# The order of three closing stores in an average pool, and a wait that one of them gets

## Chip, cores, metric

One core of a Trainium2 chip. The metric is the device time of one execution in microseconds (us).

## The reference

```python
# x: float32 (8, 32, 32, 32, 32); result: float32 (8, 32, 16, 16, 16)
window = x[:, :, 2*i:2*i+2, 2*j:2*j+2, 2*k:2*k+2]
result[:, :, i, j, k] = np.mean(window, axis=(-3, -2, -1))
```

It reads 33.55 MB, writes 4.19 MB, and adds eight numbers for each result. The kernel is a stream of DMA (copies between HBM, the chip's large memory, and the on-chip memory) with additions beside it.

## The kernel before

Ten units of rows are loaded one after the other on one DMA queue, reduced on VectorE in three steps (depth, width, height), and collected in two output buffers. Three stores on the same queue end the program.

```python
    def pool_unit(buf, t, k0, kb):
        od = kb // 8
        a = buf.rearrange("p (o dd e) -> p o dd e", o=od, dd=2)
        b = buf[:, :od * 1024]
        nc.vector.tensor_add(                                  # depth sum (line 65)
            out=b.rearrange("p (o e) -> p o e", o=od), in0=a[:, :, 0], in1=a[:, :, 1])
        # ... width sum (line 69), height sum and scale into obuf[t] (line 72)

    for t, k, kb in plan:                                      # units 0 to 9
        # ...
        nc.sync.dma_start(out=buf, in_=src)                    # loads 0 to 9
        pool_unit(buf, t, k, kb)

    nc.sync.dma_start(out=ov, in_=obuf[0])                     # store A: 2 MB, units 0 to 3

    for queue, k, n, kb in [
        (nc.sync, 0, 4, 3),                                    # store B: 1.5 MB, units 4 to 7
        (nc.sync, 12, 2, 2),                                   # store C: 0.5 MB, units 8 and 9
    ]:
        queue.dma_start(out=of[...], in_=obuf[1][...])         # cut
```

Load n is called Ln below; L8 and L9 have 2 MB each. B has 12 KB in each of the 128 partitions. After the program is compiled, the kernel also rewrites the access patterns of some DMAs and the closing of the program; the argument doesn't rest on that.

## Time and profile before

| | before |
|---|---|
| time, median of 3 runs | 91.96 us (91.9 to 92.06) |
| DMA queue | 99.2% of sixteen engines' span, 36.44 MB in the span |
| VectorE busy | 64.3 us of 86.5 (74%) |
| A issued / landed | 55.80 / 85.51 us |
| B issued / landed | 76.57 / 89.22 us |
| C issued / landed | 84.96 / 90.46 us |
| landing of L8, L9 | 75.26, 80.59 us |

Each of the sixteen DMA engines works through its own part of every transfer, in the order in which the transfers were issued. The packet records fit this: L9 is 64 packets of 32 KB, in four rounds of sixteen, one per engine, and the first packet of A starts at 79.72, when the last one of L9 has long started (78.47). A transfer has landed when its semaphore, the counter that others wait for, says so. The span of the profile ends with the last instruction; the stores land after it. Times in the text are counted from the start of the span.

### The profile page before, as it was taken

The page shows a single profiled execution, that of the slowest core. Times are in us where ns is not written, and L with a number is a line of the kernel's source. Part 1 is how long each engine was busy: PE and PEld are TensorE (multiplying, and loading weights), DVE is VectorE, ACT ScalarE, POOL GpSimd, SP SyncE. Part 2 cuts the span into 40 slices and gives each one's busy share as a digit, 9 for nine tenths or more (in the row PEclk, how much of TensorE's full clock was granted, in tenths as well). Part 3 has the DMA queues.
Part 4 walks back from the last instruction along what each step waited for, and adds up shares of the span by engine and source line. Part 5 has one row for each costly group of instructions (what it writes and reads, how often), then busy time and mean ns, then how long its engine had stood idle before and what let it go on. Part 6 is the DMA issues. An engine that isn't in the chain of part 4 may idle for free.

```text
span 86.5 us, 90 instructions
## 1 busy us (share of the span) xinstructions
DVE 64.3 (74%) x40; POOL 0.2 (0%) x4
## 2 busy tenths in 40 slices
DVE  0000049992999749992999999799689949999992
POOL 0000000000000000000000000000000000000000
DMA  8979998899979999899889998889988899899999
GB/s 242 424 333 455 485 485 379 379 455 485 485 318 424 470 485 424 364 424 606 364 364 409 591 455 364 364 364 523 568 364 364 364 485 424 349 439 303 432 439 402
DMA packets 1264, 36.44 MB, mean 421 GB/s; under 512 B 176, under 2 KB 176, under 8 KB 176
## 3 DMA queue, kind: packets, MB, share of 16 engines
q1 hardware_dynamic: 1264, 36.44, 99.2%
HBM read 33.55 MB, written 4.19 MB: 436 GB/s over the span
## 4 chain that ended last, share of the span: by engine, by line
DMA 71%; DVE 26%; issue 0%; SPq 0%; DVEq 0%
DMA tin<-in_x_dram 71%; DVE tin L65 14%; DVE tin L69 8%; DVE obuf L72 4%; SPq L85 0%; DVE dummy L72 0%; DVEq L106 0%
## 5 line engine op out<-in xcount | busy, mean ns | idle before, releaser
L65 DVE TENSOR_TENSOR tin<-tin 128x4096 f32<-128x4096 f32 (+2 forms) x10 | 35.7, 3570 | 19.9 <-DMA tin<-in_x_dram 19.9
L69 DVE TENSOR_TENSOR tin<-tin 128x2048 f32<-128x2048 f32 (+2 forms) x10 | 18.6, 1865 | 0.3
L72 DVE CUSTOM_DVE_ANT_1 obuf<-tin 128x1024 f32<-128x1024 f32 (+2 forms) x10 | 10.1, 1011 | 0.3
L72 DVE DVE_READ_ACCUMULATOR2_ANT dummy<- 128x1 f32 x10 | 0.8, 82 | 0.0
L200 POOL MEMSET const-bfloat16-1.0<- 128x1 bf16 x1 | 0.1, 101 | 0.0
L200 POOL MEMSET const-uint8-127<- 128x1 uint8 x1 | 0.1, 101 | 0.0
L200 POOL MEMSET const-float32-0.0<- 128x1 f32 x1 | 0.1, 99 | 0.2 <-issue 0.2
L200 POOL MEMSET const-float32-1.0<- 128x1 f32 x1 | 0.1, 99 | 0.0
## 6 DMA issues: line engine op xcount, KB each, us to landing
tin<-in_x_dram SPq DMA_DIRECT2D x4, 4096.0 KB, 25.6
tin<-in_x_dram SPq DMA_DIRECT2D x4, 3072.0 KB, 34.5
tin<-in_x_dram SPq DMA_DIRECT2D x2, 2048.0 KB, 25.7
out_dram<-obuf SPq DMA_DIRECT2D x1, 2048.0 KB, 29.7
out_dram<-obuf SPq DMA_DIRECT2D x1, 1536.0 KB, 12.6
out_dram<-obuf SPq DMA_DIRECT2D x1, 512.0 KB, 5.5
```

The lines of the kernel that those rows point to most:

```text
L65: nc.vector.tensor_add(out=b.rearrange("p (o e) -> p o e", o=od), in0=a[:, :, 0], in1=a[:, :, 1])
L69: nc.vector.tensor_add(out=c, in0=bv[:, :, 0], in1=bv[:, :, 1])
L72: nc.vector.tensor_tensor_reduce(out=obuf[t][:, o0:o0 + od * 256].rearrange("p (j k) -> p j k", k=16), in0=cv[:, :, 0], in1=cv[:, :, 1], s ...
L200: nc = _bacc.Bacc("TRN2", target_bir_lowering=False, num_devices=1)
```

## The change

The intent as I read it: A has been ready since unit 3 and lies in the queue behind the last loads. The change lets the stores come only when the loads are nearly through. B goes first, since it depends on unit 7, and its wait is raised by one VectorE count (one step of the semaphore that VectorE raises). For that count to exist in the right place, the depth sum of unit 8 is cut into two instructions. A stands behind B and so gets into the queue late as well.

```diff
-        nc.vector.tensor_add(
-            out=b.rearrange("p (o e) -> p o e", o=od), in0=a[:, :, 0], in1=a[:, :, 1])
+        bv = b.rearrange("p (o e) -> p o e", o=od)
+        cuts = (0, 1, od) if split else (0, od)
+        for o0, o1 in zip(cuts, cuts[1:]):
+            nc.vector.tensor_add(out=bv[:, o0:o1], in0=a[:, o0:o1, 0], in1=a[:, o0:o1, 1])
...
-        pool_unit(buf, t, k, kb)
-    nc.sync.dma_start(out=ov, in_=obuf[0])
-    for queue, k, n, kb in [(nc.sync, 0, 4, 3), (nc.sync, 12, 2, 2)]:
-        queue.dma_start(out=of[...], in_=obuf[1][...])
+        pool_unit(buf, t, k, kb, split=k == 96 and t == 1)
+    for k, n, kb in [(0, 4, 3), (12, 2, 2)]:
+        nc.sync.dma_start(out=of[...], in_=obuf[1][...])
+        if k == 0:
+            nc.sync.dma_start(out=ov, in_=obuf[0])
...
+    n, store = next(... first store of the program ...)
+    waits = [
+        copy.replace(w, wait_value=w.wait_value + 1) if w.ant_name.startswith("DVE") else w
+        for w in store.sync_info.on_wait]
+    program[n] = copy.replace(store, sync_info=mybir.SyncInfo(
+        on_wait=waits, on_update=store.sync_info.on_update))
```

## The prediction

> **What bounds the kernel now.** I read the page first, its DMA share and its chain, then the order of instructions, then stretches of the DMA stream cut at the borders between transfers, and last the single packet records.
>
> The page says that the sixteen DMA engines are full from end to end:
>
> ```profile
> DMA  8979998899979999899889998889988899899999
> ...
> q1 hardware_dynamic: 1264, 36.44, 99.2%
> HBM read 33.55 MB, written 4.19 MB: 436 GB/s over the span
> DMA 71%; DVE 26%; issue 0%; SPq 0%; DVEq 0%
> ```
>
> One queue moves everything and takes 99.2% of sixteen engines' span; the chain lies to 71% on loads. VectorE is busy 74%, so its waits are waits for loads. The 26% of DVE in the chain is an artefact of where the span stops: it ends with the last instructions at 86.5 us, while the records of the stores go on (last landing 90.46 us in the trace). What ends the run is the last packet of the DMA stream.
>
> The tail on the instruction side, from the order of instructions in time:
>
> ```profile
> 55.80 0.58 SPq L89 DMA_DIRECT2D out_dram<-obuf  x1
> ...
> 76.46 2.29 DVE L65 TENSOR_TENSOR tin<-tin 128x2048 f32<-128x2048 f32 x1
> 76.57 8.96 SPq L96 DMA_DIRECT2D out_dram<-obuf  x2
> ```
>
> Call the last two loads L8 and L9 (2 MB each), the 2 MB store A, the 1.5 MB store of 12 KB a partition B, the 0.5 MB store C. A is issued at 55.80, straight behind L9 (55.28); B at 76.57, when unit 7 is reduced; C at 84.96. The page gives issue to landing: 29.7 for A, 12.6 for B, 5.5 for C, so they land near 85.5, 89.2 and 90.5. The trace's landings are L8 75.26, L9 80.59, A 85.51, B 89.22, C 90.46. The steps are 5.33, 4.92, 3.71 and 1.24 us. A, B and C run at 426, 424 and 423 GB/s with no gap. L9 is the odd one: the same 2 MB as A, but 0.4 us more. Stretches of the stream show it (columns: stretch, its length, VectorE and GpSimd busy, clock, DMA share, GB/s of the packets that start in it):
>
> ```profile
> 62.00:69.30 7.30, 6.08 (x4) 0.00 (x0) 1.00 1.00 431
> 69.30:74.20 4.90, 3.78 (x2) 0.00 (x0) 1.00 1.00 428
> 74.20:79.70 5.50, 5.43 (x5) 0.00 (x0) 1.00 0.99 381
> 79.70:84.55 4.85, 4.75 (x6) 0.00 (x0) 1.00 1.01 432
> ```
>
> The rows are load 7, L8, L9 and A. Only L9 falls, to 381 GB/s, with the engines counted as busy throughout. The packet records say where: of 640 packets of 32 KB, 605 take 1.21 to 1.24 us; the sixteen first of the run take 1.31 to 2.00, and the only other slow ones are three started at 76.7 to 76.9 (1.31 to 1.53) and the sixteen last of L9, one per engine (1.43 to 1.95, mean 1.71). Store packets that follow are all of one length (0.611, 0.460, 0.159 us). So 1.71 - 1.23 = 0.48 us, plus (0.30 + 0.08 + 0.15)/16 = 0.03 for the three, about 0.5 in all, is lost per engine where the stream turns from reading HBM to writing it. It is the only loss in the stream after its opening, hence all that this change can win.
>
> **What the Trainium skill says.** "DMA: Bandwidth & Descriptors", section "Two DMAs through the same engine are not ordered": descriptors of one queue start in order but are pipelined, and an engine's read and write sides are separate queues. The trace agrees that order is kept (no store packet precedes its engine's last load packet). That a store waiting in the queue may already be reading while the last load is being written is the reading I take from it; the 0.5 us fits, but is no proof. Same page, "Latency and other measured facts": first byte some 0.6 us after a hardware-generated issue. Here the first load, issued at 0.00, has its first packets at 1.02 to 1.26 on fourteen engines and 1.65 and 1.89 on two; the measurement decides. "Perfetto Trace Analysis", section "DMA Instruction — HWDGE (DVE, Sync)": the issue seen in the profile starts once its semaphores are satisfied, and data movement is not in it. It agrees: B's 0.62 us issue starts 0.02 after the reduction's semaphore, its data moves eight us later. "VectorE: DVE Perf Modes", section "The TRN2 errata — SBUF-src ops pay a fixed extra latency per instruction": an fp32 add of N columns takes (N+151)/0.96 ns. Here 2048 columns take 2284 ns (formula 2291) and 1024 take 1225 ns (1224), so it agrees.
>
> **The change, part by part.**
>
> *Order.* The stores go B, A, C instead of A, B, C. Bytes and descriptors are the same. At the steady packet lengths above, eight packets an engine each, A takes 4.89, B 3.68, C 1.27, whichever is first. By itself: 0.
>
> *Time of issue.* This is the real part. A is no longer put in the queue at 55.80, because it now stands behind B. B waits for one VectorE count more, the first half of unit 8's depth sum. Unit 7's count comes at 76.55, and half the sum, 1024 columns, is about 1.21 us (line 65 takes 4426, 3358 and 2284 ns for 4096, 3072 and 2048 columns, so about 1071 ns a thousand, and 1213 for 1024). B is issued at 76.55 + 1.21 = 77.76, give or take 0.07. A follows 0.62 later, at 78.4.
>
> *Does the queue run dry?* With the opening's 1.02 to 1.26 us (two engines 1.65, 1.89) from issue to first packet, B's packets could begin at 78.78 to 79.02, on two engines at 79.4 and 79.65. L9's last packets start at 78.07 to 78.47; at 1.23 us they would end at 79.30 to 79.70. B then comes 0.05 to 0.6 us before the engine is free: just in time on most, with nothing to spare on the two slow ones. A has B's 3.68 us in front of it. C is needed when B and A are through, after 79.5 + 3.68 + 4.89 = 88.1.
>
> *VectorE.* The split makes 2284 into 2 x 1213 = 2426 ns, so 0.14 more, and a semaphore step of 0.02 to 0.03. C goes out at 84.96 + 0.17 = 85.13 with its engines taken until 88: 3 us of slack, hidden.
>
> *Sum.* If nothing of the store is in the queue while L9's last packets are filled, up to 0.50 comes back. B still comes somewhat before the end of L9 and some loss will stay, and its own first packet may have to fill an empty pipe. I count about two thirds: 0.50 x 0.65 = 0.33, with the split hidden. 91.96 - 0.33 = 91.63.
>
> **The rivals.**
>
> 1. *The turn costs what it costs.* The 0.5 us comes from changing direction (reads of HBM drained, writes begun), not from an early store. Then it is paid at any issue time: 91.9 to 92.0. For it: the opening packets too take 0.1 to 0.8 us too long, so filling the pipe costs such an amount when nothing is ahead. Against it: the late part is the last load packet, whose landing is really late, not the first store packet.
> 2. *The queue runs dry.* If B needs over 1.6 us to its first packet (its 3 KB rows make four times the write descriptors), all engines stand idle for the difference. At 2 us that is some 0.3 us idle on top of a cleared turn, a time of 91.8 to 92.0; if the turn is paid as well, 92.3. For it: the two slow engines of the opening. Against it: the delay is chosen at half of a sum and not a whole one, which suggests that somebody sought this edge.
> 3. *The issue of B disturbs the loads.* B's descriptors are made at 76.57 to 77.19, just before the three slow packets end. If that slows the loads, a later issue only shifts it: no change, 91.96. Against it: the issues at 20.1, 29.8, 39.5, 49.2, 55.3 and 55.8 have no slow packet after them.
> 4. *All of it comes back:* 91.96 - 0.51 = 91.45. There is nothing else to win: 37.75 MB at the steady 430 GB/s are 87.8 us, and the rest lies in the opening and the closing, which are untouched.
>
> **Range and chances.** The four ways span 91.4 to 92.3; the three runs of before spread by 0.16. I put 0.55 on a gain of 0.2 to 0.5, 0.3 on no change and 0.15 on a loss: 91.63, eight times in ten 91.3 to 92.05. Two per cent is 1.84 us, over three times what the stream loses at all, so faster by that is out; a dry queue of 1.84 us would take 3.5 us from issue to first packet. 0.01, 0.98, 0.01.
>
> **What would show it.** In the changed profile B's issue should stand near 77.8 and A's near 78.4; the two half sums at 1.2 us each; C's issue near 85.1 with a shorter issue to landing, near 5.0. The stretch of L9 should go back from 381 to over 410 GB/s and its landing from 80.59 to about 80.2, and the last landing from 90.46 to about 90.1. It is wrong if L9's last packets are again 1.7 us long with B issued at 77.8 (rival 1 or 3), or if they are short but a gap, or long first packets of B, stand behind them (rival 2). The idle time of VectorE should not move before 76 us.

## More of the kernel before

All runs told here were at a granted clock of 1.00. Every kernel was timed on the same chip and in the same rounds as the kernel before; the groups of runs were on different chips, on which the kernel before took 91.91 to 91.97 us.

One way of cutting the trace has to be known for what follows. The view of stretches adds up the packets that start in a stretch, so its GB/s depend on where the stretch is cut. The fair cut for a transfer is from its own first packet to the first packet of the next one. For L9 in the kernel before this is 74.28 to 79.72 (columns: stretch, length, VectorE, GpSimd, clock, DMA share, GB/s):

```profile
74.27:79.71 5.44, 5.37 (x5) 0.00 (x0) 1.00 1.00 386
```

## The result

| | before | after |
|---|---|---|
| time, median of 6 runs | 91.93 us (91.74 to 92.09) | 91.29 us (91.27 to 91.31) |
| ratio of the fast runs | | 0.993 (95%: 0.9917 to 0.9943) |
| landing of L8, L9 | 75.26, 80.59 | 75.22, 80.11 |
| last landing | 90.46 | 89.90 |

A ratio here is the mean time of one kernel's fast runs over that of the other's in the same rounds, so not quite the ratio of the medians. The change is worth 0.64 us, 0.7%, clear of the noise and inside the 2%. The predicted 91.63 is 0.34 too high, and the measured time lies 0.01 under the range.

The instructions of the changed kernel from unit 8 on, in order of time (start, length, engine, line, operation):

```profile
76.41 2.48 DVE L68 TENSOR_TENSOR tin<-tin 128x1024 f32<-128x1024 f32 x2
77.66 0.62 SPq L93 DMA_DIRECT2D out_dram<-obuf  x1
78.33 0.58 SPq L98 DMA_DIRECT2D out_dram<-obuf  x1
...
85.11 0.57 SPq L93 DMA_DIRECT2D out_dram<-obuf  x1
```

B is issued at 77.66 (predicted 77.76), A at 78.33 (78.4), C at 85.11 (85.13). The page gives their ways from issue to landing:

```profile
out_dram<-obuf SPq DMA_DIRECT2D x1, 2048.0 KB, 10.3
out_dram<-obuf SPq DMA_DIRECT2D x1, 1536.0 KB, 6.2
out_dram<-obuf SPq DMA_DIRECT2D x1, 512.0 KB, 4.8
```

A was 29.7 us under way and is now 10.3; all but some five of these are waiting in the queue. The stream itself, cut at the first packets of L8, L9, B, A and C:

```profile
69.50:74.40 4.90, 4.02 (x2) 0.00 (x0) 1.00 1.00 428
74.40:79.30 4.90, 4.80 (x6) 0.00 (x0) 1.00 1.00 428
79.30:83.00 3.70, 3.67 (x4) 0.00 (x0) 1.00 1.01 425
83.00:87.86 4.86, 2.01 (x4) 0.00 (x0) 1.00 1.01 432
```

L9 now takes the same 4.90 us as L8, where it took 5.44. The packet records agree: the sixteen last packets of L9, one per engine, took 1.43 to 1.95 us before (mean 1.71) and take 1.227 now, every one. B's first packets start 0.00 us after the load packets end (mean over the engines); neither a gap nor a long first packet stands there. Of the 0.56 us by which the last landing comes earlier, 0.48 is there at L9's landing (0.04 of it at L8's already). By the packet records the engine that ends L9 last does so at 79.68 for 80.28, 0.60 earlier, so the gain lies in L9 and not in the stores behind it. That last engine sets the time: in the twelve profiles told here that have neither an idle gap nor an added transfer or turn, six with an early store and six with late ones, the run took 11.57 to 11.63 us more than its end. The timed runs say 0.64 and not 0.56 because the profiled run of before (91.85) was one of the faster ones.

### The profile page after: what moved, and what is told of

It is laid out like the page before. It is cut to its first block, busy times and chain, and to the rows that moved or that the text cites. A ratio compares the mean times of both kernels' runs of the same rounds, so it can differ in the third digit from the quotient of the medians.

```text
span 86.7 us, 91 instructions
## 1 busy us (share of the span) xinstructions
DVE 64.5 (74%) x41; POOL 0.2 (0%) x4
## 4 chain that ended last, share of the span: by engine, by line
DMA 70%; DVE 26%; issue 0%; SPq 0%; DVEq 0%
DMA tin<-in_x_dram 70%; DVE tin L68 14%; DVE tin L71 8%; DVE obuf L74 4%; SPq L87 0%; DVE dummy L74 0%; DVEq L105 0%
## 5 line engine op out<-in xcount | busy, mean ns | idle before, releaser
L68 DVE TENSOR_TENSOR tin<-tin 128x4096 f32<-128x4096 f32 (+3 forms) x11 | 35.9, 3260 | 19.9 <-DMA tin<-in_x_dram 19.9
## 6 DMA issues: line engine op xcount, KB each, us to landing
out_dram<-obuf SPq DMA_DIRECT2D x1, 2048.0 KB, 10.3
```

The source lines that it names most:

```text
L68: nc.vector.tensor_add(out=bv[:, o0:o1], in0=a[:, o0:o1, 0], in1=a[:, o0:o1, 1])
```

## The experiments

The first theory: a store that lies in the queue while the last load packets run delays those packets; late issue removes the loss, and the order is nothing. Rivals were: the turn from loads to stores costs 0.5 us at any time; the issue of B at 76.6 disturbs the loads; the split or B's place in front helps by itself; the queue could be held until it runs dry. Below, "loss" is the sum over L9's slowed packets of the time over 1.227 us, divided by the sixteen engines; only packets slowed by more than 0.06 us count. It is a mean over the engines.

### The parts of the change

**split_only.** The kernel before with unit 8's sum split (`split=k == 96 and t == 1`), nothing else.

> The kernel before with unit 8's depth sum cut in two and nothing else moved. Theory (the gain comes from the store not lying in the queue while the last load's packets run): no gain, 91.9 to 92.0, VectorE 0.14 to 0.19 us longer and hidden, the last sixteen load packets still 1.4 to 1.95 us (mean about 1.7). Rival (the split itself helps, by another pace of VectorE beside the DMA): 91.3.

Measured: 91.96, beside 91.91 for the kernel before (ratio 0.9998, 0.9981 to 1.0016). The split by itself does nothing. One thing was missed: in this profile the slowed packets stood one round earlier (mean 1.45 in L9's third round, 1.25 in the fourth). It is a stretch of time, between 77 and 80, and not only the last packet that suffers. The loss is also smaller here, 0.23, though the profiled run took 92.00: packets of the 3 MB loads took up to 2.03 us where none took over 1.83 in the kernel before, L9 began later (74.65 for 74.28), and its last engine ended at 80.43. So the mean loss alone does not give the time.

**a_first_held.** The old order with the changed kernel's hold, now on A.

```diff
+    nc.sync.dma_start(out=ov, in_=obuf[0])
     for k, n, kb in [(0, 4, 3), (12, 2, 2)]:
...
-        if k == 0:
-            nc.sync.dma_start(out=ov, in_=obuf[0])
...  # A gets B's VectorE wait + 1
```

> Stores in the old order A, B, C, but A held back until the first half of unit 8's sum, so that it is issued near 77.7 and B right behind it. Theory (issue time is all, order is nothing): 91.3 within 0.1, the last load packets all 1.23 us. Rival (B's place in front, or its short rows, is what helps): at or near 91.9. A's issue is a little shorter than B's, so the first packets cannot come later than in the changed kernel.

Measured: 91.34 (ratio 0.9932), A issued at 77.71, all load packets 1.227 us. As expected: with the same issue time, the order is worth nothing.

**b_first_no_hold.** The new order; the wait is not raised (`wait_value + 0`).

> Stores in the new order B, A, C without the extra wait: B issued near 76.5, its first packets ready near 77.6 by the opening's 1.0 us, before the last load packets start at 78.1. Theory: the loss is back, 91.7 to 92.0, last load packets mean 1.5 to 1.75 us. Rival one (only a store queued long before, since 55.8, does harm): 91.3. Rival two (the three slow packets of the kernel before at 76.7 to 76.9 came from B's issue at 76.6): those three are slow here too.

Measured: 91.34 (ratio 0.9932), B issued at 76.55, A at 77.22, no slow load packet. Here the theory failed. It wanted most of the loss back, and nothing came back. So B issued three us before the loads end (79.52, mean) does no harm, and rival one was right in so far as what harms must be a store queued earlier (how much earlier, the runs further down show). Rival two fails: with B issued at 76.55 the packets that start from 76.9 on are not slow.

**hold_whole.** B waits for both halves (`wait_value + 2`).

> As the changed kernel, but B waits for both halves of the sum, issued near 78.9. With 1.0 to 1.7 us from issue to first packet it arrives at 79.9 to 80.6, while the loads end at 79.3 to 79.7. Theory: last load packets 1.23 us, then the engines stand idle 0.5 to 0.9 us, so 91.8 to 92.2. Rival (issue to first packet is shorter when the chip is warm, or the engines drain something anyway): the gap is under 0.3 and the time 91.3 to 91.5.

Measured: 92.26 (ratio 1.0029, 1.0012 to 1.0045), slightly over the expected range. B was issued at 78.93. The stretch of L9, to B's first packet:

```profile
74.30:80.20 5.90, 5.76 (x7) 0.00 (x0) 1.00 0.83 355
```

Here the DMA share falls to 0.83, where the kernel before kept 1.00: the engines stand idle. Before, they counted as busy with packets that were too long. The load packets end at 79.49 and the engines' first store packets start at 80.27 (both means): 0.78 us idle. The very first one starts at 80.21, 1.28 us after the issue.

### Early store or second issue?

In the kernel before two things came together: A lay in the queue since 55.8, and B was issued at 76.57, behind A and beside the loads. The next runs take them apart.

**a_early_b_late.** The kernel before, B's wait raised by three counts, to the end of unit 8.

> The kernel before, A queued at 55.8 as ever, but B held until unit 8 is reduced, so issued near 80.7 instead of 76.6, long after the last load packet has started and 3.9 us before A is through (84.6). The earlier idea, that a store lying behind the last load delays its packets, expects the loss unchanged: 91.8 to 92.0, slow 32 KB packets between 77 and 80. New theory (what costs is the issue of a second store at 76.6 while the first one has lain behind the loads for long): no slow load packets after the opening, 91.3 to 91.4.

Measured: 91.91 beside 91.95 (ratio 0.9991, 0.9971 to 1.0011). B was issued at 80.74, and 28 load packets from 76.95 on were slow all the same (loss 0.53). B's issue, and the stretch from L9's first packet to A's:

```profile
80.74 4.78 SPq L96 DMA_DIRECT2D out_dram<-obuf  x2
```

```profile
74.50:79.68 5.18, 5.11 (x5) 0.00 (x0) 1.00 1.05 405
```

The stretch ends with the first engine to be through; the last one ended L9 at 80.33. The "new theory" of that expectation is refuted, and with it the third rival of the prediction. The first idea holds in so far as the early A is the cause.

**a_first_no_hold.** As a_first_held with A's wait at B's own value.

> Old order A, B, C, A issued near 76.5 without the hold and B right behind it near 77.0. If issuing B second, behind a waiting store and beside running loads, is what costs, then slow load packets between 77.5 and 80 and 91.8 to 92.0. If only a store queued some twenty us before does harm, no slow packet and 91.3, as with B first and no hold.

Measured: 91.38 (ratio 0.9935). A was issued at 76.59, B behind it at 77.00. Nine packets were slow, loss 0.10. So nearly nothing, but not quite: this issue time lies on the edge.

**a_after_unit6**, **a_after_depth7** and **a_after_width7.** The same kernel with A's wait three, two and one counts lower.

```diff
-        copy.replace(w, wait_value=w.wait_value + 1)
+        copy.replace(w, wait_value=w.wait_value - 3)   # unit 6 done; - 2: depth sum of unit 7; - 1: its width sum
```

> Old order A, B, C, A issued when unit 6 is reduced, near 69.2, that is, with loads 8 and 9 whole in front of it; B at 76.6 as in the kernel before. Under the idea that a long waiting store does harm by itself, or that B's issue behind a waiting store does: 91.8 to 92.0 with slow packets between 77 and 80. Under the idea that it must be queued at 55.8, while four loads are ahead of it: 91.3.

> Old order A, B, C; A issued when unit 7's depth sum is done, near 73.8, so in the queue near 74.8, about 4.5 us before the loads end; B at 76.6. Known: issued at 69.35 the loss is whole (91.92), at 76.6 nearly none (91.38). If the reading side of the DMA engines runs some two packets ahead of the writing side and the harm is done where it meets a waiting store, the last two rounds of load packets (from 76.8) are the ones slowed, so a store there at 74.8 still meets it: 91.8 to 91.95. If the harm fades in proportion to the time in the queue: about 91.6.

> As the run before it, A issued when unit 7's width sum is done, near 75.6, in the queue near 76.6, just before the first slowed packets of the kernel before would start (76.7 to 77). Two-packets-ahead reading: part of the loss or most of it, 91.6 to 91.9. If only the very start of the last load matters (74.3): 91.35.

Measured: 91.92 (ratio 0.9994), 91.97 (1.0000) and 91.91 (0.9994), with losses of 0.44, 0.43 and 0.47. It matters not whether A comes at 55.8 or at 75.57; the loss is whole. The instructions of the last of these and the stretch of its L9:

```profile
75.57 0.36 SPq L92 DMA_DIRECT2D out_dram<-obuf  x1
...
76.57 0.63 SPq L94 DMA_DIRECT2D out_dram<-obuf  x1
```

```profile
74.26:79.62 5.36, 5.26 (x6) 0.00 (x0) 1.00 1.00 391
```

One microsecond later, with A issued at 76.59 (a_first_no_hold):

```profile
74.36:79.37 5.01, 4.91 (x6) 0.00 (x0) 1.00 1.00 419
```

Here is the whole curve of issue times of the first store. Where the loads are not slowed, they end at 79.2 to 79.9:

| first store issued at | kernel | loss in L9's packets | idle after them | median |
|---|---|---|---|---|
| 55.79 to 55.83 | before (first group of runs), a_early_b_late, split_only | 0.52, 0.53, 0.23 | 0 | 91.93, 91.91, 91.96 |
| 69.35 | a_after_unit6 | 0.44 | 0 | 91.92 |
| 73.78 | a_after_depth7 | 0.43 | 0 | 91.97 |
| 75.57 | a_after_width7 | 0.47 | 0 | 91.91 |
| 76.54 to 76.59 | b_first_plain, b_first_no_hold, a_first_no_hold | 0.01, 0.00, 0.10 | 0.00 | 91.30, 91.34, 91.38 |
| 77.66 to 77.71 | after, a_first_held | 0.00 | 0.00 | 91.29, 91.34 |
| 78.93 | hold_whole | 0.00 | 0.78 | 92.26 |
| 79.21 | hold_three_quarters (told below) | 0.00 | 1.03 | 92.37 |

It is a step and not a slope: nearly all of the loss disappears between 75.6 and 76.6, some three us before the loads end.

### What about the early store does the harm?

**two_turns.** The kernel before with a quarter of A ahead of L9.

```diff
+        if (t, k) == (1, 112):
+            nc.sync.dma_start(out=ov[:, :1024], in_=obuf[0][:, :1024])
         nc.sync.dma_start(out=buf, in_=src)
...
-    nc.sync.dma_start(out=ov, in_=obuf[0])
+    nc.sync.dma_start(out=ov[:, 1024:], in_=obuf[0][:, 1024:])
```

> The kernel before with a quarter of A, 0.5 MB, issued ahead of the last load, so that the stream turns from loads to stores twice and back once; the rest of A follows L9 as before. If the turn itself costs, the last sixteen packets of load 8 (near 73.5 to 75) are slow as well by about 0.5 us and the run is 0.5 us or more slower than the kernel before, 92.4 or more, with the refill after the small store on top. If the issue at 76.6 is what costs, load 8's last packets are 1.23 us and only those in flight near 77.5 to 79.5 are slow: 91.9 to 92.3.

Measured: 92.85 beside 91.95 (ratio 1.0098, 1.0076 to 1.0119). L8, now the load with a store behind it, against the untouched L9 rounds:

```profile
69.50:75.16 5.66, 4.60 (x2) 0.00 (x0) 1.00 1.00 371
```

L8's third and fourth rounds of packets have means of 1.55 and 1.67, a loss of 0.76; the small store's packets take 0.178 for 0.159 (0.15 over its eight), and L9's first round 1.39 (0.17). So the store behind L8 costs as well, and going back to loads costs too. But the second turn, from L9 to the rest of A, which lay in the queue since 55.94, cost nothing: L9's last two rounds have means of 1.224 and 1.223. I didn't expect that and have no tested reason; it shows that a waiting store does not do harm at every turn. The terms add up to 1.08 against the 0.52 of the kernel before, 0.56 more of the 0.90 measured. The rest lies mostly in the spread of the engines, which end L9 over 1.08 us instead of 0.56: the last one ends at 82.40 for 80.28, 2.12 later, of which 1.27 are the small store's own length (8 packets of 0.159), so 0.85 of the 0.98 us between the two profiled runs.

**sbuf_copy_early** and **hbm_copy_early.** The changed kernel with 0.5 MB more queued at 55.8 behind L9: once a copy inside the on-chip memory, once a copy from HBM to HBM. The stores stay late.

```diff
+    nc.sync.dma_start(out=scratch[:, :], in_=obuf[0][:, :1024])                       # sbuf_copy_early
+    nc.sync.dma_start(out=of[P * 12 * KF:]..., in_=xf[:P * 4 * KF]...)                # hbm_copy_early
```

> The changed kernel with 0.5 MB copied from on-chip buffer to on-chip buffer, issued at 55.8 behind the last load; the stores stay as in the changed kernel. Result right, the copy is not used. If what slows the last load packets is a waiting transfer that reads the on-chip memory (its data coming in ahead), the last two rounds of 32 KB packets are slow, about 0.5 us an engine, and the time is 91.3 plus 1.2 for the copy plus 0.5, less what it overlaps: 92.7 to 93.1. If writing to HBM is needed for the harm, they are 1.23 us and the time is 92.4 to 92.6.

> The changed kernel with 0.5 MB copied from HBM to HBM at 55.8 behind the last load, into the region that the last store overwrites afterwards, so the result is right. If the harm is in reading the on-chip memory early, the last load packets keep 1.23 us. If it is in turning to HBM writes, they are slow by about 0.5 us as in the kernel before.

Measured: 93.05 (ratio 1.0122) and 92.56 (1.0064), both beside 91.94. L9 in the first, then in the second:

```profile
74.39:79.62 5.23, 5.13 (x6) 0.00 (x0) 1.00 1.02 401
```

```profile
74.40:79.29 4.89, 4.79 (x6) 0.00 (x0) 1.00 1.00 429
```

With the on-chip copy 24 load packets from 76.84 on are slow (loss 0.41), as behind the kernel's own store. With the HBM copy there is not one. Writing to HBM is thus not needed for the harm, and having a transfer in the queue is not enough for it; what the harmful ones have in common is that they read the on-chip memory. One reservation: the HBM copy moves one packet of 32 KB per engine, the on-chip copy eight of 4 KB, and I have no run that changes the shape alone.

### Does the hold do anything?

**after_again**, **b_first_plain** and **hold_three_quarters**, on one chip. b_first_plain is the order B, A, C alone, without the split and the raised wait:

```diff
-        pool_unit(buf, t, k, kb, split=k == 96 and t == 1)
+        pool_unit(buf, t, k, kb, split=False)
...  # the block that raises the first store's wait is deleted
```

> The changed kernel unaltered, for a comparison on the same chip: 91.3 within 0.05.

> The changed kernel without split and without hold: the order B, A, C alone. If the order alone (which takes A out of the queue until 77.2) brings all: 91.25 to 91.35, within 0.05 of the changed kernel. If hold and split have a part of their own: 91.35 to 91.45 and a few slow load packets near 78 to 80 in its profile.

> The hold lengthened to three quarters of the sum, B issued near 78.4. In the kernel held for the whole sum B was issued at 78.93 and its first packet started at 80.21, 1.28 us later, while the loads ended at 79.25 to 79.66. At 78.4 the first packets would start near 79.65 at the earliest: a gap of 0.0 to 0.4 us, 91.5 to 91.8. If it is still 91.3, the window is wider than I think.

Measured: 91.36 for the changed kernel (91.27 to 91.38; 0.01 over what was expected), 91.30 for the plain order (91.28 to 91.37), beside 91.97 for the kernel before; ratios 0.9932 and 0.9930. The plain order does the same with less. L9 in its profile:

```profile
74.33:79.22 4.89, 4.82 (x5) 0.00 (x0) 1.00 1.01 429
```

hold_three_quarters missed its purpose: in its trace VectorE's semaphore steps at 77.87 (first piece of the sum) and 79.20 (its end), and the middle one of the three pieces has no count of its own, so "two counts more" meant the end of the whole sum. B was issued at 79.21, the engines stood idle for 1.03 us, and it took 92.37 (ratio 1.0040). It is a second, later hold_whole. Whether three quarters would still be free is open.

## Why the prediction was wrong

1. *What bounds, and where the loss is:* right. In the two profiles the turn at L9 was the only loss after the opening, and what came back came back there. L9's last packets went from a mean of 1.71 to 1.227.
2. *Direction and kind:* right. The early A is the cause (a_early_b_late, a_first_held).
3. *The size, "0.50 x 0.65 = 0.33":* this is the step that failed. I put a third of the loss down as staying, because "B still comes somewhat before the end of L9" and "its own first packet may have to fill an empty pipe". Both terms are zero. The load packets show a loss of 0.00 with B issued at 77.66, and still 0.00 to 0.01 with it issued at 76.54 (0.10 with A in front at 76.59), so B may come before the end of L9, by three us, and still no loss stays. B's first packets take 0.467 us, like its later ones. With the whole 0.51 the sum gives 91.45; the remaining 0.16 has two parts. 0.11: the 0.51 was read from a profiled run that took 91.85, and I took it off the median of 91.96. 0.05: the 0.51 is a mean over the engines, but the time follows the engine that ends L9 last, and this one ended 0.60 earlier (the stores gave 0.04 back, so the last landing came 0.56 earlier). So "all that this change can win" was bounded by the wrong quantity.
4. *"Time of issue. This is the real part":* half right. That A leaves the queue is what counts, and the order alone does that. The split and the hold, with which my working dealt most, are worth nothing (91.36 with, 91.30 without). The condition of the sum, "if nothing of the store is in the queue while L9's last packets are filled", is not what decides: in b_first_no_hold B was issued at 76.55, and it took 91.34.
5. *The split:* right that it is hidden. It costs VectorE 2.48 us for 2.29, 0.19 where I had 0.14 (the "1071 ns a thousand" are for 1024 columns), and C 0.15 us.
6. *The rivals:* the turn doesn't cost what it costs (1). B's issue doesn't disturb (3). The dry queue (2) is real, but one step further on: at 78.93 it costs 0.78 us of idle time. Rival 4, all of it comes back, was the right one, and I gave the range too little room on its side.
7. *The spread:* the runs of before lie within 91.73 to 92.39 in all groups, those of the changed kernel within 91.27 to 91.38. In the six profiles with an early store the last engine ended L9 at 80.25 to 80.44 and the times went with it (91.83 to 92.02). The mean loss did not go with them: 0.43 in the slowest, 0.52 in the second fastest. What spreads the engines stays open.

What stays open is the mechanism inside the engine. Shown is, for A and for the on-chip copy, that a transfer which reads the on-chip memory and is issued behind L9 at 75.57 or before lengthens the load packets that start from about 76.8 on, and that a store issued from 76.54 on does so hardly or not at all (a late copy was not run). That the reading side of an engine gets through with L9 at about that time, and takes a waiting store's data in ahead of load data still on the way, would fit, but is not shown, and the second turn of two_turns, where nothing was lost, isn't explained by it. There the waiting store had packets of 12 KB where A has 16, and the engines stood further apart; neither was tested by itself.

## What to carry to other kernels

In a stream that is bound by its DMA queue, a store that is ready early should not be queued early behind the last loads: in the six kernels here with a store issued by 75.57 and a single turn that cost 0.2 to 0.5 us of load packets (mean over the engines) and some 0.6 us of time, in a place where the engines count as fully busy. The second turn of two_turns is an exception, so measure it; whether a second queue would help was not tried. Put a store in front that becomes ready late by itself, and the early one behind it. The other side of the window is near: first packets came 1.28 us after an issue with nothing else left in the queue (hold_whole), so by that figure (an estimate) the changed kernel's issue at 77.66 left some 0.3 us until the first engines, done at 79.25 to 79.3, would stand idle, while the plain order left 1.4 us for the same time.

## What the Trainium skill lacked or had wrong

- "DMA: Bandwidth & Descriptors", section "Rules for kernel authors", advises to issue a DMA early to overlap it with compute. That row names no limit. For a store on the queue of the loads the runs show one: issued at 75.57 or before 91.9 us, at 76.54 to 77.71 91.3 us.
- The same page says nothing of what it costs to go from loads to stores within a queue: 0.2 to 0.5 us per engine here with the store waiting, 0.00 to 0.10 with the store issued in the last three us; and nothing of the difference between a waiting transfer that reads on-chip memory (loss 0.41) and one that reads HBM (0.00).
- The same page, section "Latency and other measured facts", gives some 0.6 us to the first byte. The first packet started 1.28 us after the start of the issue in hold_whole, where the queue held nothing else, and 1.01 us after it at the opening of the changed kernel.
- "Perfetto Trace Analysis", section "Identifying the Most-Contended Engine", calls the occupancy of the DMA engines misleading, for their number. It doesn't say that packets which take too long count as busy: in the kernel before the share was 1.00 in the stretch where 2 MB took 5.44 us instead of 4.90.
